# Picking expert numbers for four heads at once, with halving additions on GpSimd, in a hybrid decoder block

## The chip, the core and the metric

The kernel runs on one core of a Trainium2 chip. The core has five engines with a queue of instructions each: TensorE (PE in the views, with PEld for its weight loads), VectorE (DVE), ScalarE (ACT), GpSimd (POOL) and SyncE (SP, which here only issues DMAs). Each queue is worked off in order; the engines wait for one another at semaphores. The metric is the time of one execution on the device in microseconds, as the median of several runs. Before the change it is 3037.69 us (three runs, 3037.05 to 3041.81).

## What is computed

One decoder block over 16 meta tokens and 1024 tokens of width 1024: a convolution branch and a latent attention branch, joined by a projection, and then a PEER layer, which mixes 128 x 128 = 16384 experts. The change is in the PEER layer, which works on chunks of 128 tokens (C = 128):

```python
def one(xb):
    q = (xb @ wq).reshape(C, PEER_HEADS, 2, PEER_DK_HALF)              # 8 heads
    s = jnp.einsum('chpd,hpnd->chpn', q, keys)                         # 2 x 128 key scores
    sv, si = lax.top_k(s, 16)
    cand = sv[:, :, 0, :, None] + sv[:, :, 1, None, :]
    cidx = si[:, :, 0, :, None] * N_KEYS + si[:, :, 1, None, :]
    top_s, sel = lax.top_k(cand.reshape(C, PEER_HEADS, 256), 16)
    eidx = jnp.take_along_axis(cidx.reshape(C, PEER_HEADS, 256), sel, axis=-1)
    g = jax.nn.softmax(top_s, axis=-1)
    u = u_tab[eidx]
    act = jax.nn.gelu(jnp.einsum('chkd,cd->chk', u, xb), approximate=False)
    return jnp.einsum('chk,chkd->cd', g * act, v_tab[eidx])
```

Every token so uses 8 x 16 = 128 rows of u_tab and of v_tab, and `eidx` holds their numbers.

## The kernel before

The 1024 tokens are eight chunks of 128, in groups SC of 1, 1, 2, 2 and 2 chunks. A hand-written list of steps, ORDER, sets the order in which the code is written: B is attention of a group, C its output projection and key scores (`mix_out`), S the pick of experts (`select`), T the turning of their numbers and weights (`turn`), E an expansion (`expand`), G and the loop D the rest. A scheduler then orders the instructions of each engine anew, by that order as priority and by its own estimate of when operands and buffers are there. So a change in one place can move instructions in others.

**select** (L610 to L655) works on one chunk. Of the 256 sums of two scores only 50 can be among the best 16 (NCAND; the first 8 are among NC1 = 20), and they are laid out as `cand`, with their expert numbers as `cidx`. DVE finds the best 16 and their places among the 50. To turn a place into an expert number, L631 to L639 go over the heads one by one (HB = 1) and over two halves of the 16: DVE compares the 8 places with 0 to n-1, which gives a one-hot tile `eq` (L637, 20 x 8 or 50 x 8 elements of f16); POOL multiplies it by `cidx` into `ep` (L638); DVE sums over the candidates into `ef` (L639). That is 16 of each of the three per chunk, with two buffers for each tile.

Chunks 0 to 3 (GATHER) then fetch the picked rows: `gather_u` issues 128 indirect DMAs per chunk on POOL's queue, a row for each token into `ug` (three buffers, L688), and DVE multiplies each with the tokens `xn` and sums (L691, written as ujunk). `gather_v` does the same with v_tab into `vg` (seven buffers, L714), four at a time, and PE adds each four, weighted, by 16 matmuls into `gv` (L718, a "step" below, 32 for each chunk). The sum is added to the stream `ht` and normalised by `finish`. All these are written late (steps G32 and D0), and the scheduler draws them forward into free places.

Chunks 4 to 7 (DENSE) are instead multiplied with all experts. `expand` (L739 to L769) makes a 128 x 128 table of weights per token: DVE writes one-hot tiles `two` and `one` (L753, L754) of 8 tokens, then the products `ah` (L755) and `al` (L756), the latter in every other round on POOL (ALP); PE multiplies them into `pg` (L761, L762), ACT copies to `st` (L764), and DMAs write the table `g_d`. There are 16 rounds per chunk. `one` has a single buffer, so the next round's `one` waits until `al` has read it; the others have two.

The loop of `dense` (L810 to L835) takes four rows of experts in each of 32 groups: PE multiplies u (`pa`) and v (`pv`), 96 matmuls each per group (pv goes to `acc` by L835), and after each row of experts some of the gather is written in (RATE). At the end `finish` normalises chunks 4 to 7.

## Time and profile before

| what | value |
|---|---|
| median of three runs | 3037.69 us |
| profiled execution, its own time | 3034.4 us |
| its span, first to last instruction | 3032.6 us |
| granted PE clock, mean over the span | 0.908 |
| PE busy, of the span | 85% |
| DVE busy | 71% |
| POOL busy | 52% |
| ACT busy | 33% |
| bytes moved by DMA | 858 MB, 283 GB/s |

All rows that are read below come from that one execution, so a sum is made against 3034.4 us and then carried to the median. In the views, a row of an engine names the line of code, the operation, the tile written and the tiles read, the shape, and a count; times are us, the durations of single instructions ns. Busy time of overlapping instructions is counted once. "Waits" are idle time of an engine, put down to what ended it.

### The profile page before, as it was taken

The numbers are of one execution on the slowest core, as the hardware profiler recorded it, in microseconds if no ns is written. First come the engines' busy times: TensorE is split into PE (matmuls) and PEld (weight loads), VectorE is DVE, ScalarE is ACT, GpSimd is POOL, SyncE is SP. The second block draws the span as 40 slices with busy tenths as digits, with TensorE's granted clock in tenths as the row PEclk, the third lists the DMA queues.
The fourth block names the chain that finished last, engine by engine and source line by source line (L and its number), as shares of the span: only waits on it lengthen the run. The fifth ranks groups of instructions, "written<-read, shape, count | busy, mean of one in ns | idle before, by whom it ended". The sixth has DMA issues, their size and how long they took to land.

```text
span 3032.6 us, 40483 instructions
## 1 busy us (share of the span) xinstructions
PE 2591.0 (85%) x13295; PEld 1932.6 (64%) x13295; DVE 2165.6 (71%) x4917; ACT 1009.9 (33%) x2200; POOL 1589.2 (52%) x1608
## 2 busy tenths in 40 slices
PE   6878669897876756558998999999999999999996
PEld 6775547776643534336877777777777777776663
DVE  4888857999998999876877766666676656653332
ACT  5435325352520433443222222322232322232221
POOL 5885453534568668662333544544555444534444
PEclk9888858898897877668999999999999999999998
DMA  4114789896788996998888999999999999978886
GB/s 141 46 49 144 227 257 322 261 295 225 246 280 288 314 305 228 315 307 316 300 297 285 326 356 348 332 347 335 346 334 345 337 343 339 352 282 318 311 308 215
DMA packets 372563, 858.36 MB, mean 283 GB/s; under 512 B 37952, under 2 KB 134400, under 8 KB 368256
## 3 DMA queue, kind: packets, MB, share of 16 engines
q0 software_dynamic: 147456, 536.94, 50.9%
q1 hardware_dynamic: 216528, 295.68, 28.7%
q10 hardware_dynamic: 8368, 23.15, 2.1%
q8 instruction: 105, 1.72, 0.2%
q14 instruction: 106, 0.87, 0.1%
HBM read 798.92 MB, written 56.71 MB: 282 GB/s over the span
## 4 chain that ended last, share of the span: by engine, by line
PE 49%; DVE 17%; DMA 12%; issue 4%; POOL 3%; ACT 1%; POOLq 0%; DVEq 0%; ACTq 0%; SPq 0%
PE pv L178 19%; PE pa L178 18%; DMA ug<-in_dram,ei 9%; PE gv L718 7%; DVE ujunk L691 4%; DVE ef L639 2%; DMA vg<-in_dram,eT 1%; PE op L564 1%; DVE two L753 1%; DVE eq L637 1%; DVE ah L755 1%; POOL vg L714 1%; DVE one L754 1%; POOL ug L688 1%; POOL al L756 1%
## 5 line engine op out<-in xcount | busy, mean ns | idle before, releaser
L714 POOL DMA_INDIRECT vg<-in_dram,eT x512 | 559.5, 1093 | 652.6 <-PE gv L718 520.0
L688 POOL DMA_INDIRECT ug<-in_dram,ei x512 | 553.7, 1081 | 584.4 <-DVE ujunk L691 299.6
L691 DVE SCALAR_TENSOR_TENSOR ujunk<-ug,xn 128x1024 bf16<-128x1024 f32 x512 | 638.4, 1247 | 149.4 <-DMA ug<-in_dram,ei 139.1
L835 DVE TENSOR_TENSOR acc<-acc,pv 128x512 f32<-128x512 f32 x256 | 171.9, 685 | 203.5 <-PE pv L178 176.1
L718 PE MATMUL gv<-vg,wd 128*32 128x512 f32 x2048 | 275.6, 653 | 37.5 <-DMA vg<-in_dram,eT 37.4
L178 PE MATMUL pv<-v_0h,wh 128*128 128x512 f32 x512 | 201.3, 398 | 23.9 <-ACT wh L821 16.9
L178 PE MATMUL pv<-v_1l,wh 128*128 128x512 f32 x512 | 200.9, 394 | 3.7 <-DVE v_1l L784 3.7
L178 PE MATMUL pa<-xdh,u_1l 128*128 128x512 f32 x512 | 200.8, 392 | 2.5 <-DVE u_1l L784 2.5
L178 PE MATMUL pa<-xdh,u_0h 128*128 128x512 f32 x512 | 202.1, 395 | 0.3 <-ACT st L764 0.3
L178 PE MATMUL pa<-xdl,u_0h 128*128 128x512 f32 x512 | 201.3, 393 | 0.0
L178 PE MATMUL pa<-xdh,u_0l 128*128 128x512 f32 x512 | 201.2, 393 | 0.0
L178 PE MATMUL pa<-xdh,u_1h 128*128 128x512 f32 x512 | 201.0, 393 | 0.2 <-ACT u_1h L783 0.2
L178 PE MATMUL pa<-xdl,u_1h 128*128 128x512 f32 x512 | 200.4, 391 | 0.0
L178 PE MATMUL pv<-v_0l,wh 128*128 128x512 f32 x512 | 200.3, 395 | 0.0
L178 PE MATMUL pv<-v_1h,wl 128*128 128x512 f32 x512 | 199.9, 392 | 0.0
L178 PE MATMUL pv<-v_1h,wh 128*128 128x512 f32 x512 | 196.5, 396 | 2.8 <-DVE acc L835 2.8
L783 ACT ACTIVATE u_1h<-u_1r 128x512 fp32r<-128x512 f32 x128 | 80.7, 631 | 349.6 <-PE pa L178 251.1
L178 PE MATMUL pv<-v_0h,wl 128*128 128x512 f32 x512 | 194.7, 395 | 0.8 <-DVE wl L822 0.8
L764 ACT ACTIVATE st<-pg 128x256 f32<-128x256 f32 x256 | 130.1, 644 | 190.0 <-PE pg L762 140.7
L783 ACT ACTIVATE u_0h<-u_0r 128x512 fp32r<-128x512 f32 x128 | 80.8, 631 | 322.4 <-PE pa L178 244.9
L761 PE MATMUL pg<-ah,two 128*128 128x128 f16 x512 | 98.0, 271 | 98.2 <-DVE ah L755 82.8
L784 DVE TENSOR_TENSOR u_0l<-u_0r,u_0h 128x512 fp32r<-128x512 f32 x128 | 88.5, 692 | 126.6 <-ACT u_0h L783 89.7
(449 smaller groups left out, 5910.1 us busy)
## 6 DMA issues: line engine op xcount, KB each, us to landing
g_d<-st SPq DMA_DIRECT2D x32, 1024.0 KB
u_0r<-in_dram SPq DMA_DIRECT2D x128, 256.0 KB
u_1r<-in_dram SPq DMA_DIRECT2D x128, 256.0 KB
gt<-g_d SPq DMA_DIRECT2D x32, 1024.0 KB
v_0r<-in_dram SPq DMA_DIRECT2D x128, 256.0 KB
v_1r<-in_dram SPq DMA_DIRECT2D x128, 256.0 KB
wo<-in_dram SPq DMA_DIRECT2D x80, 256.0 KB
wq<-in_dram SPq DMA_DIRECT2D x80, 256.0 KB
```

Of the source, the lines that this page charges most:

```text
L178: PE.matmul(dst, l, r, start=first and j == 0, stop=last and j == 2)
L564: PE.matmul(pb, MT[:, k, j * P:(j + 1) * P], w[k // 2][:, k % 2], start=k == 0, stop=k == KD - 1)
L639: V.tensor_reduce(e[:, h:h + HB, ks], pr.rearrange("p h c k -> p h k c"), axis=AX.X, op=OP.add)
L688: G.indirect_dma_start(out=ug, out_offset=None, in_=u_tab, in_offset=bass.IndirectOffsetOnAxis(ap=ei[:, j:j + 1], axis=0))
L691: V.scalar_tensor_tensor(junk, ug, 1.0, xn, op0=OP.mult, op1=OP.mult, accum_out=dots[:, j:j + 1])
L714: G.indirect_dma_start(out=vg[j], out_offset=None, in_=v_tab, in_offset=bass.IndirectOffsetOnAxis(ap=eT[:, t:t + 1], axis=0))
L718: PE.matmul(acc[32 * j:32 * j + 32, 512 * n:512 * n + 512], w[:, j, 32 * i:32 * i + 32], vg[j][:, 512 * n:512 * n + 512], start=q == 0 and ...
L761: PE.matmul(pg[:, k], two[:, a, :, b], ah[:, a, :, b], start=True, stop=False)
L764: A.activation(st[i][:, :, r0 + r:r0 + r + 4].rearrange("p a b -> p b a"), pg[:, :, i * NK // 2:(i + 1) * NK // 2], AF.Copy, scale=1.0 / G ...
L783: A.activation(hi, raw, AF.Copy)
L784: V.tensor_tensor(lo, raw, hi.bitcast(F32), op=OP.subtract)
L835: V.tensor_tensor(a, a, pv, op=OP.add)
```

## The change

`select` takes a number of heads at a time from `dim.hb`: 1 for chunk 0 as before, 4 for the others. For these, a tile holds 4 x 20 x 8 or 4 x 50 x 8 elements and has one buffer (`dim.eb`). After the multiplication POOL folds the candidates: it adds the upper half onto the lower while more than 13 are left, so 20 become 10 by one addition and 50 become 25 and then 13 by two. DVE sums the remaining 10 or 13. Per chunk there are 4 comparisons, 4 multiplications, 6 additions and 4 reductions. In `expand` the tile `one` gets a second buffer.

```diff
-        for h in range(0, H, HB):
+        hb = dim.hb
+        for h in range(0, H, hb):
             for i, n in enumerate((NC1, NCAND)):
                 ks = slice(8 * i, 8 * i + 8)
-                sh = [P, HB, n, 8]
-                eq = sel.tile(sh, F16, name=f"eq{c}_{h}_{i}", tag=f"eq{i}", bufs=2)
-                pr = sel.tile(sh, F32, name=f"ep{c}_{h}_{i}", tag=f"ep{i}", bufs=2)
-                V.tensor_tensor(eq, tf[:, h:h + HB, None, ks].broadcast_to(sh), iota_c[:, None, :n].broadcast_to(sh), op=OP.is_equal)
-                G.tensor_tensor(pr, eq, cidx[:, h:h + HB, :n, None].broadcast_to(sh), op=OP.mult)
-                V.tensor_reduce(e[:, h:h + HB, ks], pr.rearrange("p h c k -> p h k c"), axis=AX.X, op=OP.add)
+                sh = [P, hb, n, 8]
+                eq = sel.tile(sh, F16, name=f"eq{c}_{h}_{i}", tag=f"eq{i}", bufs=dim.eb)
+                pr = sel.tile(sh, F32, name=f"ep{c}_{h}_{i}", tag=f"ep{i}", bufs=dim.eb)
+                V.tensor_tensor(eq, tf[:, h:h + hb, None, ks].broadcast_to(sh), iota_c[:, None, :n].broadcast_to(sh), op=OP.is_equal)
+                G.tensor_tensor(pr, eq, cidx[:, h:h + hb, :n, None].broadcast_to(sh), op=OP.mult)
+                while hb > 1 and n > 13:
+                    m = n // 2
+                    G.tensor_tensor(pr[:, :, :m], pr[:, :, :m], pr[:, :, n - m:n], op=OP.add)
+                    n -= m
+                V.tensor_reduce(e[:, h:h + hb, ks], pr[:, :, :n].rearrange("p h c k -> p h k c"), axis=AX.X, op=OP.add)
...
-                                    for n, b in (("one", 1), ("two", 2), ("ah", 2), ("al", 2))]
+                                    for n, b in (("one", 2), ("two", 2), ("ah", 2), ("al", 2))]
...
-    dim = SimpleNamespace(nw=1, nk=1, wraw=WRAW0)
+    dim = SimpleNamespace(nw=1, nk=1, wraw=WRAW0, hb=1, eb=2)
...
-    dim = SimpleNamespace(nw=NW, nk=NC, wraw=WRAW)
+    dim = SimpleNamespace(nw=NW, nk=NC, wraw=WRAW, hb=H // 2, eb=1)
```

In the changed kernel the multiplication stands in L638, the additions in L641, the reduction in L643; other lines of the profile before are one lower above these and four higher below (the ug issue is L692, the vg issue L718, the products of `expand` L757 to L760).

The scheduler makes of this the following. POOL's queue at the pick of chunk 4, before (ep and eq are named by head and half, ug and vg by the row that they fetch; the last number is the buffer's):

```order
L638 TENSOR_TENSOR ep_0_0_7299<-eq_0_0_7298,cidx_7229 128x160
L638 TENSOR_TENSOR ep_0_1_7304<-eq_0_1_7303,cidx_7229 128x400
L638 TENSOR_TENSOR ep_1_0_7309<-eq_1_0_7308,cidx_7229 128x160
L638 TENSOR_TENSOR ep_1_1_7314<-eq_1_1_7313,cidx_7229 128x400
L714 DMA vg_101_12419<-in_dram,eT_2889 128x1024
L714 DMA vg_6_12489<-in_dram,eT_2889 128x1024
L714 DMA vg_38_12491<-in_dram,eT_2889 128x1024
L638 TENSOR_TENSOR ep_2_0_7319<-eq_2_0_7318,cidx_7229 128x160
L714 DMA vg_70_12493<-in_dram,eT_2889 128x1024
L688 DMA ug_22_12437<-in_dram,ei_4618 128x1024
L638 TENSOR_TENSOR ep_2_1_7324<-eq_2_1_7323,cidx_7229 128x400
```

and the same queue at the same pick after:

```order
L638 TENSOR_TENSOR ep_0_0_7137<-eq_0_0_7136,cidx_7067 128x640
L638 TENSOR_TENSOR ep_0_1_7143<-eq_0_1_7142,cidx_7067 128x1600
L692 DMA ug_22_12059<-in_dram,ei_4564 128x1024
L641 TENSOR_TENSOR ep_0_0_7137<-ep_0_0_7137 128x4x80
L692 DMA ug_23_12063<-in_dram,ei_4564 128x1024
L641 TENSOR_TENSOR ep_0_1_7143<-ep_0_1_7143 128x4x200
L718 DMA vg_103_12193<-in_dram,eT_2889 128x1024
L718 DMA vg_8_12264<-in_dram,eT_2889 128x1024
L718 DMA vg_40_12266<-in_dram,eT_2889 128x1024
L718 DMA vg_72_12268<-in_dram,eT_2889 128x1024
L692 DMA ug_24_12127<-in_dram,ei_4564 128x1024
L641 TENSOR_TENSOR ep_0_1_7143<-ep_0_1_7143 128x4x96
```

Before, a multiplication is all that a reduction needs of POOL; after, the last addition of a half stands behind seven more issues.

DVE's queue in the expansion of chunk 7, before (one, two, ah and al are named by quarter of the chunk and first token of the round; L691 is the product of a gathered row):

```order
L754 TENSOR_TENSOR one_2_0_11083<-io,gd_10258 128x1024
L753 TENSOR_TENSOR two_2_0_11084<-io,gd_10258 128x1024
L755 TENSOR_TENSOR ah_2_0_11085<-one_2_0_11083,gd_10258 128x1024
L756 TENSOR_TENSOR al_2_0_11086<-one_2_0_11083,gd_10258 128x1024
L753 TENSOR_TENSOR two_2_8_11114<-io,gd_10258 128x1024
L691 SCALAR_TENSOR_TENSOR ujunk,dots_12008<-ug_79_13950,xn_12006 128x1024
L754 TENSOR_TENSOR one_2_8_11113<-io,gd_10258 128x1024
L753 TENSOR_TENSOR two_2_16_11144<-io,gd_10258 128x1024
L755 TENSOR_TENSOR ah_2_8_11115<-one_2_8_11113,gd_10258 128x1024
L754 TENSOR_TENSOR one_2_16_11143<-io,gd_10258 128x1024
```

and after:

```order
L758 TENSOR_TENSOR one_1_24_10671<-io,gd_9880 128x1024
L758 TENSOR_TENSOR one_2_0_10705<-io,gd_9880 128x1024
L757 TENSOR_TENSOR two_1_24_10672<-io,gd_9880 128x1024
L759 TENSOR_TENSOR ah_1_24_10673<-one_1_24_10671,gd_9880 128x1024
L695 SCALAR_TENSOR_TENSOR ujunk,dots_11630<-ug_90_13958,xn_11628 128x1024
L758 TENSOR_TENSOR one_2_8_10735<-io,gd_9880 128x1024
L695 SCALAR_TENSOR_TENSOR ujunk,dots_11630<-ug_91_13962,xn_11628 128x1024
L695 SCALAR_TENSOR_TENSOR ujunk,dots_11630<-ug_92_13982,xn_11628 128x1024
L759 TENSOR_TENSOR ah_2_0_10707<-one_2_0_10705,gd_9880 128x1024
```

The tile one is now written a round ahead, and the gather is eleven rows further at the same place.

The end of DVE's queue, before (L724 adds the last gathered chunk to ht, L736 normalises):

```order
L784 TENSOR_TENSOR v_3_1l<-v_3_1r,v_3_1h 128x512
L835 TENSOR_TENSOR acc<-acc,pv_1_0_26309 128x512
L835 TENSOR_TENSOR acc<-acc,pv_1_1_26323 128x512
L835 TENSOR_TENSOR acc<-acc,pv_1_2_26337 128x512
L835 TENSOR_TENSOR acc<-acc,pv_1_3_26351 128x512
L724 TENSOR_TENSOR ht_25387<-ht_25387,gv_22294 128x1024
L736 SCALAR_TENSOR_TENSOR ht_25387<-ht_25387,os_25391,gfin 128x1024
L736 SCALAR_TENSOR_TENSOR acc<-acc,os_26366,gfin 128x1024
```

and after:

```order
L822 TENSOR_TENSOR ge_25820<-ge_25820,gt_25649 128x512
L728 TENSOR_TENSOR ht_25009<-ht_25009,gv_21916 128x1024
L826 TENSOR_TENSOR wl_25824<-ge_25820,wh_25823 128x512
L740 SCALAR_TENSOR_TENSOR ht_25009<-ht_25009,os_25013,gfin 128x1024
L839 TENSOR_TENSOR acc<-acc,pv_0_0_25851 128x512
L839 TENSOR_TENSOR acc<-acc,pv_0_1_25865 128x512
L839 TENSOR_TENSOR acc<-acc,pv_0_2_25879 128x512
```

The last gathered chunk is finished ahead of the last group's eight additions to acc, where it stood behind them. On PE the last three steps of gv stood behind the last pv; now 96 pv stand behind the last gv.

## Rows read from the trace of the kernel before

**Rows 1.** The page: busy us, share of the span, instructions of each engine

```profile
PE 2591.0 (85%) x13295; PEld 1932.6 (64%) x13295; DVE 2165.6 (71%) x4917; ACT 1009.9 (33%) x2200; POOL 1589.2 (52%) x1608
```

**Rows 2.** Busy time by stretch: us, engines (instructions), PE clock, DMA share, GB/s

```profile
735.00:800.00 65.00, 56.08 (x278) 44.52 (x276) 65.00 (x204) 26.48 (x74) 44.54 (x58) 0.87 0.65 206
875.00:1000.00 125.00, 72.81 (x347) 43.39 (x348) 109.47 (x374) 15.93 (x37) 104.55 (x119) 0.77 0.83 289
1100.00:1217.00 117.00, 63.08 (x395) 41.42 (x395) 115.82 (x351) 38.93 (x76) 91.36 (x98) 0.69 0.81 271
1217.00:1365.00 148.00, 79.17 (x629) 49.37 (x629) 117.06 (x165) 62.56 (x125) 95.40 (x72) 0.64 0.93 309
...
1400.00:1760.00 360.00, 339.29 (x1471) 267.34 (x1472) 285.44 (x479) 103.96 (x185) 143.83 (x130) 0.99 0.87 302
1760.00:2990.00 1230.00, 1228.16 (x6019) 890.22 (x6021) 712.61 (x1146) 341.86 (x573) 579.78 (x539) 1.00 0.92 330
```

**Rows 3.** Groups by line and shape: busy us, mean ns, idle before and releaser

```profile
L638 POOL TENSOR_TENSOR ep<-eq,cidx 128x400 f32<-128x400 f16 x64 | 60.2, 944 | 15.1 <-DVE eq L637 14.8
...
L639 DVE TENSOR_REDUCE ef<-ep 128x8 f32<-128x400 f32 x64 | 55.4, 865 | 0.7 <-POOL ep L638 0.7
...
L638 POOL TENSOR_TENSOR ep<-eq,cidx 128x160 f32<-128x160 f16 x64 | 44.9, 703 | 18.4 <-DVE eq L637 17.5 <-DVE tv L604 0.3 <-DVE gs L645 0.2
...
L637 DVE TENSOR_TENSOR eq<-tf,iota_c 128x160 f16<-128x160 f16 x64 | 32.5, 507 | 0.0
...
L639 DVE TENSOR_REDUCE ef<-ep 128x8 f32<-128x160 f32 x64 | 27.3, 428 | 5.7 <-POOL ep L638 5.7
...
L637 DVE TENSOR_TENSOR eq<-tf,iota_c 128x400 f16<-128x400 f16 x64 | 26.3, 411 | 0.0
```

**Rows 4.** POOL's float sums and products, lines L327, L341: minimum, median, maximum ns

```profile
L327 POOL TENSOR_TENSOR first<-first,ct x60: 443/460/1477, 39.8 to 192.5; 128x128 f32<-128x128 f32 x60
...
L341 POOL TENSOR_TENSOR y<-y,gln x8: 1265/1293/2358, 204.8 to 343.9; 128x512 f32<-128x512 f32 x8
```

**Rows 5.** Timeline, DVE, 1284 to 1298 us: start, us, instruction [idle before, releaser]

```profile
1292.34 0.69 DVE L754 TENSOR_TENSOR one<-io,gd 128x1024 f16<-128x1024 f16 x1 [6.49 <-POOL al L756]
...
1293.55 0.68 DVE L755 TENSOR_TENSOR ah<-one,gd 128x1024 f16<-128x1024 f16 x1
...
1297.10 2.37 DVE L755 TENSOR_TENSOR ah<-one,gd 128x1024 f16<-128x1024 f16 x1
```

**Rows 6.** Timeline, POOL, 1284 to 1299 us

```profile
1286.96 0.94 POOL L714 DMA_INDIRECT vg<-in_dram,eT  x1 [0.30 <-issue]
...
1290.40 1.91 POOL L756 TENSOR_TENSOR al<-one,gd 128x1024 f16<-128x1024 f16 x1
1296.21 2.72 POOL L756 TENSOR_TENSOR al<-one,gd 128x1024 f16<-128x1024 f16 x1 [3.90 <-DVE one L754]
```

**Rows 7.** Waits, 1217 to 1365 us: engine and line, for what; us, times, longest

```profile
DVE one L754 <- POOL al L756: 26.0, 5, 7.0
```

**Rows 8.** Waits, 1400 to 1760 us

```profile
DVE ujunk L691 <- DMA ug<-in_dram,ei: 61.6, 40, 7.3
```

**Rows 9.** Chain that ended last, 2950 to 3033 us: start, us, what

```profile
2982.03 7.07 PE pv L178 x30
2989.10 1.98 PE gv L718 x16
...
2991.21 4.14 DMA vg<-in_dram,eT
...
2997.57 5.36 DMA vg<-in_dram,eT
...
3006.87 5.14 DMA vg<-in_dram,eT
...
3015.49 1.23 DVE ht L724
...
3026.07 1.28 DVE acc L736
```

More of the change, by code (lines that the diff above doesn't have):

```diff
@@ L51 @@
 NC1 = sum(na * nb for _, na, _, nb in BLOCKS[:4])
-HB = 1
 SC = [(0, 128), (128, 128), (256, 256), (512, 256), (768, 256)]
```

## The prediction

> **What bounds the kernel now.** I read the page first: PE is busy for 85% of the span, VectorE (DVE) for 71%, ScalarE (ACT) for 33% and GpSimd (POOL) for 52% [rows 1]. Such shares mix stages, so the second view is busy time by stretch [rows 2]. From 1760 to 2990 us PE is busy for 1228 of 1230 us at a granted clock of 1.00 (the 2.4 GHz level): there only fewer or shorter matmuls help, and the change removes none of them. The picture before that is another. In 735 to 800 us, where experts of chunks 2 and 3 are picked, DVE has no idle time at all; in 1100 to 1217 us (chunks 6 and 7) it is busy for 115.8 of 117 us; in 875 to 1000 us (chunks 4 and 5) DVE has 109.5 and POOL 104.6 of 125 us, so both are near their limit. In 1217 to 1365 us (the last two expansions into one-hot tiles) no engine is full: DVE and POOL wait for each other. The third view is the groups by line and shape, for what the changed lines cost [rows 3]; the fourth the timelines of DVE and POOL in one expansion round [rows 5, 6]; the last is the end of the chain [rows 9].
>
> **Part 1, picks for four heads at once, on DVE.** Per chunk, before: eight reductions of 160 elements at 428 ns and eight of 400 at 865 ns [rows 3], 10.3 us. The two sizes give (865 - 428)/240 = 1.82 ns an element and a fixed 137 ns. After: two of 320 elements (4 x 10 x 8) and two of 416 (4 x 13 x 8), 0.72 and 0.89 us, together 3.2 us. That is 7.1 us a chunk; chunk 0 keeps the old form, so seven chunks give 50 us. The comparisons cost 8 x (507 + 411) ns = 7.3 us a chunk [rows 3]. After, there are four of 640 and 1600 elements. A free one of 1024 elements of f16 takes 0.68 us [rows 5], and with 411 ns at 400 that makes 0.51 and 0.93 us, 2.9 us a chunk: 31 us less in all. But a two-input DVE instruction that meets a GpSimd one waits for it: the same 1024-element product takes 0.68 us at 1293.55 and 2.37 us at 1297.10, while the 2.72 us POOL product that began at 1296.21 runs [rows 5, 6]. The multiplications that the new comparisons meet are longer (below, 1.3 and 2.8 us). If each of the four meets one in full, 8.2 us a chunk come on top, and the comparisons cost 27 us more than before. I take the middle of these means, half a multiplication each on average: 4.1 us a chunk, 2 us gained in all, and keep +31 and -27. DVE so loses between 23 and 81 us of work; I take 52.
>
> The Trainium skill (SBUF — State Buffer, section "Who interferes with whom") says of the pair of ports which VectorE and GpSimd share that a VectorE instruction with two SBUF inputs contends with a GpSimd instruction that reads SBUF, and that reductions never do on trn2. By that rule the work moves from instructions which are never blocked to additions that block others, and the time would be that of the second rival; the pair of products at 1293.55 and 1297.10 agrees with the rule.
>
> **On POOL.** Before, 8 x (703 + 944) ns = 13.2 us a chunk [rows 3]. After, two multiplications of 640 and two of 1600: from 944 ns at 400 elements and 1.91 us at 1024 [rows 3, 6] 1.55 ns an element, 1.3 and 2.8 us, 8.2 us a chunk. No halving addition stands in the trace; the nearest are other float adds and products in SBUF, 443 ns at 128 elements and 1265 ns at 512 at their fastest [rows 4], 2.14 ns an element. Each half then takes 0.86 us (320), 1.88 (800) and 0.99 (384): 7.5 us a chunk. In sum 15.7 us, 2.5 more than before, 18 us over seven chunks; at the slowest row (2.36 us for 512, 1.9 times) 66 us. I take 30, nearer to the fast end, since DVE blocks less often with fewer instructions.
>
> **What of it is on the path.** Where DVE was full, POOL becomes the next bound: 735 to 800 us had 44.5 us of POOL work and gets some 9 more, 53 of 65; 875 to 1000 us gets 113 of 125; 1100 to 1217 us 100 of 117 [rows 2]. Idle POOL time gone entirely, these give back 12, 12 and 17 us, and chunk 1 perhaps 1: at most 42 us. If DVE stays the bound all of its 52 to 81 us counts; if POOL's waits for gathers stay as they are, nothing does. Reductions hardly wait for POOL now (5.7 and 0.7 us in 128 times [rows 3]); after, each waits for a chain of one multiplication and one or two additions, with gathers in between: in the GpSimd table the second addition of the first half stands behind four vg and three ug issues. I take 30 us off.
>
> **Part 2, the second one tile.** In 1217 to 1365 us DVE waits 26.0 us in 5 places for POOL's product before it may overwrite one [rows 7]; one of them is the 6.49 us before 1292.34 [rows 5], while POOL does four vg issues of 0.94 us, 0.3 us apart, before its product [rows 6]. The buffer takes this wait away, 26 us at most. What comes next is POOL itself, busy for 95.4 of 148 us [rows 2] plus about 54 gaps of 0.3 us, 111 us. And the scheduler uses the room: counted in the order, 68 gathers stand between the 17th and the last POOL product of the expansions where 54 stood. 14 x 1.24 us = 17 us more, 129 of 148. DMA engines are at 0.93 there, 309 GB/s [rows 2]; 14 x 0.52 MB at that rate would be 24 us by itself. So between 19 us faster and 24 us slower; I take 4 faster, since the DMA engines moved 330 GB/s at 0.92 in 1760 to 2990 us, and the wait is there in the trace.
>
> **Part 3, what the pulled-forward gathers give at the end.** This is the largest sure term. Before, three of the gather's matmul steps (16 matmuls each) stand behind the last pv: PE waits 4.14, 5.36 and 5.14 us for their rows, then ht is added, and five normalisations follow [rows 9]. From the step that starts at 2989.10 us to the end of the span are 43.5 us. After, by the order, all gv stand before the last 96 pv, and ht of chunk 3 is finished ahead of them. What is left from the same point is PE work: four steps at 1.9 us and 15 pv at 7.07/30 us [rows 9], 11 us; then the finish. Now 10.6 us lie between ht and the last of five products and 6.5 us from that product's start to the end; two of the five are left to do then, 4 and 6.5, 10.5 us. 43.5 - 21.5 is 22 us; one more step of 1.9 us is already done before the dense loop (32 instead of 31). Total 24 us. 96 pv at 0.236 us are 22.6 us, enough to cover the 17 us from ht to the end. If the gather rows come later than the order assumes, the waits return inside the loop and as little as 8 us is left.
>
> In 1400 to 1760 us PE has 339 of 360 us, for DVE waits 61.6 us for ug rows [rows 2, 8]. Counted in the order, DVE has 98 ug to take in the first six groups of the dense loop after, and 108 in the first seven before, so the same share is lost: I count nothing.
>
> **Sum.** The profiled execution took 3034.4 us with a span of 3032.6. 3034.4 - 30 - 4 - 24 = 2976. It lies 3.3 us under the median of the runs shown (3037.69), so the forecast is 2980 us.
>
> **Rivals.** (1) **Reductions wait for POOL**, slower. 28 reductions stand in DVE's in-order queue; behind each stand the products with xn (ujunk) that free the ug buffers, and the one-hot products that PE and ACT wait for. For: the chain in the GpSimd table, two multiplications, three additions and seven issues, is some 16 us long. Against: between the second comparison of that half and its reduction the order puts 33 rows of other DVE work, and today POOL waits for DVE, not the other way. DVE saves 52; with a wait w each the stages change by 28w - 52, and the tail gives back 24, so it decides from w = 2.7 us. At 4 us: 3034 + 60 - 24 + 3 = 3073; at 3.2 us 3052. (2) **POOL's longer work blocks DVE**: every comparison and many ujunk and one-hot products wait; DVE saves 23 instead of 52, the path perhaps 5. 3034 - 5 - 24 + 3 = 3008. Rows 5 and 6 speak for it; against it, blocking is there already (160 elements take 507 ns by mean, 400 take 411 [rows 3]) in 112 comparisons, and 28 are left. (3) **DVE remains the bound throughout**: 60 from the picks, 15 from the one tile, 24 at the end: 2938. For: DVE full in three stretches; against: POOL's 104.6 of 125. (4) **Gathers pulled forward are paid where they are put**, DMA at its limit in 1217 to 1365 us: 20 to 24 us lost there, the tail and nothing else gained: 3034 to 3040, no change.
>
> **Chances.** Forecast (2955 to 3000) 0.52, blocking (3000 to 3028) 0.16, DVE bound (below 2955) 0.13, no change 0.09, waits 0.10. The range 2942 to 3035 leaves out the far halves of the third and first rival. A measurement of this kernel tells about 0.2%, 6 us. Faster 0.81, same 0.09, slower 0.10.
>
> **What would show it.** In the profile after: reductions x28 near 0.7 and 0.9 us; additions near 0.9, 1.9 and 1.0 us; little idle time before L643 on POOL's account (much of it: rival 1); comparisons near 0.5 and 0.9 us (2 us and more: rival 2); no DVE wait of 6 us before one; PE full from 1360 to 1375 us on, not from 1400; and no gv between the last pv and the end. The prediction is wrong if the dense loop comes no earlier, or if PE waits for vg in the last 100 us.

## The result and the profile after

The changed kernel takes 3058.99 us (median of 6 runs), the kernel before 3042.47 us (6 runs beside it): ratio 1.0062, 95% interval 1.0049 to 1.0076. That is **slower** by 17 us by the medians and 19 us by the ratio: small, but clear of the noise. The forecast was 2980 us and faster; the range ended at 3035. For most single instructions and at the end of the program the forecast held; what failed lies between 560 and 1480 us. The two profiled executions differ by 22 us, a little more than the medians.

The page after, busy us of each engine (as [rows 1]):

```profile
PE 2590.0 (85%) x13295; PEld 1930.5 (63%) x13295; DVE 2179.4 (71%) x4749; ACT 1011.4 (33%) x2200; POOL 1605.6 (53%) x1566
```

VectorE has 168 instructions fewer and is busy for 14 us *longer*. The changed lines alone do not say why. Groups by line and shape of the kernel after, as [rows 3]: busy us, mean ns, idle before and releaser.

```profile
L638 POOL TENSOR_TENSOR ep<-eq,cidx 128x1600 f32<-128x1600 f16 x14 | 44.4, 3170 | 1.7 <-DVE ef L643 1.6
...
L641 POOL TENSOR_TENSOR ep<-ep 128x800 f32<-128x800 f32 x14 | 27.5, 1964 | 0.3
L638 POOL TENSOR_TENSOR ep<-eq,cidx 128x640 f32<-128x640 f16 x14 | 21.2, 1512 | 5.5 <-DVE eq L637 2.9 <-DVE mx L503 1.8 <-DVE ef L643 0.6
L637 DVE TENSOR_TENSOR eq<-tf,iota_c 128x1600 f16<-128x1600 f16 x14 | 18.0, 1287 | 2.4 <-POOL ep L638 2.4
L641 POOL TENSOR_TENSOR ep<-ep 128x384 f32<-128x384 f32 x14 | 15.8, 1126 | 0.2
L637 DVE TENSOR_TENSOR eq<-tf,iota_c 128x640 f16<-128x640 f16 x14 | 12.6, 902 | 4.2 <-POOL ep L638 4.2
L643 DVE TENSOR_REDUCE ef<-ep 128x32 f32<-128x416 f32 x14 | 12.5, 893 | 8.0 <-POOL ep L641 8.0
L641 POOL TENSOR_TENSOR ep<-ep 128x320 f32<-128x320 f32 x14 | 12.3, 877 | 0.2
L643 DVE TENSOR_REDUCE ef<-ep 128x32 f32<-128x320 f32 x14 | 10.0, 713 | 0.0
```

Most prices of the forecast are met here: reductions 0.71 and 0.89 us, additions 0.88, 1.96 and 1.13 (0.86, 1.88 and 0.99 were forecast). Multiplications are some 15% longer than forecast, 1.51 and 3.17 us for 1.3 and 2.8, and comparisons, at 0.90 and 1.29, lie between the free price of 0.51 and 0.93 and the longer one that was taken. The reductions wait 8.0 us in all for POOL, so the first rival is out. The same kind of row for the dot products `ujunk`, from 560 to 1430 us, before and then after:

```profile
L691 DVE SCALAR_TENSOR_TENSOR ujunk<-ug,xn 128x1024 bf16<-128x1024 f32 x175 | 226.1, 1292 | 22.3 <-DMA ug<-in_dram,ei 20.5 <-issue 0.8 <-DVE sx L605 0.7
```

```profile
L695 DVE SCALAR_TENSOR_TENSOR ujunk<-ug,xn 128x1024 bf16<-128x1024 f32 x183 | 272.3, 1488 | 49.0 <-DMA ug<-in_dram,ei 47.2 <-issue 1.3
```

A line that the change does not touch: its mean rose from 1292 to 1488 ns, and the idle time ahead of it from 22 to 49 us, on the account of the gathers. Together these are 73 us, of which some 10 are eight more of them; the reductions and comparisons saved 50 and 19 us. The timelines show one of these instructions. First VectorE (DVE), then POOL, kernel after, around 591 us (start, us, instruction):

```profile
591.16 5.14 DVE L695 SCALAR_TENSOR_TENSOR ujunk<-ug,xn 128x1024 bf16<-128x1024 f32 x1
596.24 0.08 DVE L695 DVE_READ_ACCUMULATOR ujunk<-ug,xn 128x1 f32 x1
```

```profile
591.32 0.86 POOL L641 TENSOR_TENSOR ep<-ep 128x320 f32<-128x320 f32 x1
592.14 0.18 POOL L139 TENSOR_TENSOR fs<-fs,pow_c 128x1 f32<-128x1 f32 x1
592.29 2.92 POOL L638 TENSOR_TENSOR ep<-eq,cidx 128x1600 f32<-128x1600 f16 x1
596.59 0.99 POOL L692 DMA_INDIRECT ug<-in_dram,ei  x1 [1.37 <-DVE ujunk L695]
```

A free `ujunk` takes 1.22 us; this one is held for the whole of an addition and of the four-head multiplication behind it, although it began first, and ends 1.1 us after them. The next gather is issued only then: it waits 1.37 us for the buffer that `ujunk` gives back. So VectorE loses twice, once held and once waiting for rows that were asked for late.

Busy time by stretch after (columns as [rows 2]; the third line, which ended with the expansions at 1365 us, now runs to 1412 us, and its work is not the same: the last reduction of the picks starts at 1277.6 us, where it started at 1216.8 before):

```profile
875.00:1000.00 125.00, 74.07 (x356) 44.74 (x356) 98.05 (x317) 12.91 (x31) 98.24 (x95) 0.77 0.76 255
1100.00:1217.00 117.00, 61.60 (x468) 41.94 (x466) 113.87 (x374) 45.19 (x94) 79.68 (x62) 0.70 0.88 289
1217.00:1412.00 195.00, 106.30 (x749) 67.76 (x750) 162.99 (x213) 70.67 (x141) 147.35 (x119) 0.65 0.89 294
1400.00:1760.00 360.00, 321.99 (x1404) 256.68 (x1403) 282.15 (x471) 106.76 (x191) 130.82 (x120) 0.96 0.87 299
1760.00:2990.00 1230.00, 1224.75 (x6001) 883.58 (x6000) 704.35 (x1131) 340.45 (x570) 574.90 (x541) 1.00 0.93 333
```

The last accumulation of the dense loop's first group stands at 1438.6 us before and 1483.2 after (L835, L839): 44.6 us late. The loop then takes 1556.7 and 1562.9 us to its last accumulation. The wait of `one` fell as meant ([rows 7], 26.0 us in 5 places), and the wait for `ug` in the loop's first part is as before ([rows 8], 61.6 us in 40). Waits, 1217 to 1412 us and 1400 to 1760 us, kernel after:

```profile
DVE one L758 <- POOL al L760: 8.1, 4, 2.8
```

```profile
DVE ujunk L695 <- DMA ug<-in_dram,ei: 62.5, 43, 3.6
```

The end behaves as forecast: the last step of `gv` starts at 3019.90 us, ahead of the last 96 `pv`, and one accumulation and its normalisation are all that follow the loop (timeline of PE, then two pieces of the chain that ended last; compare [rows 9]).

```profile
3019.90 1.92 PE L722 MATMUL gv<-vg,wd 128*32 128x512 f32 x16
```

```profile
3045.43 0.69 DVE acc L839
...
3048.31 1.28 DVE acc L740
```

From the last accumulation to the end of the span 37.3 us became 8.7.

### The profile page after: what moved, and what is told of

It is laid out like the page before. It is cut to its first block, busy times and chain, and to the rows that moved or that the text cites. A ratio compares the mean times of both kernels' runs of the same rounds, so it can differ in the third digit from the quotient of the medians.

```text
span 3054.9 us, 40224 instructions
## 1 busy us (share of the span) xinstructions
PE 2590.0 (85%) x13295; PEld 1930.5 (63%) x13295; DVE 2179.4 (71%) x4749; ACT 1011.4 (33%) x2200; POOL 1605.6 (53%) x1566
## 5 line engine op out<-in xcount | busy, mean ns | idle before, releaser
L718 POOL DMA_INDIRECT vg<-in_dram,eT x512 | 558.5, 1091 | 673.6 <-PE gv L722 534.5
L692 POOL DMA_INDIRECT ug<-in_dram,ei x512 | 553.8, 1082 | 577.8 <-DVE ujunk L695 308.6
L695 DVE SCALAR_TENSOR_TENSOR ujunk<-ug,xn 128x1024 bf16<-128x1024 f32 x512 | 674.2, 1317 | 168.8 <-DMA ug<-in_dram,ei 159.1
L839 DVE TENSOR_TENSOR acc<-acc,pv 128x512 f32<-128x512 f32 x256 | 171.9, 684 | 197.9 <-PE pv L177 167.2
L722 PEld LDWEIGHTS gv<-vg,wd 128*32 128x32 f32 x2048 | 57.3, 116 | 207.7 <-issue 143.3
```

The source lines that it names most:

```text
L692: G.indirect_dma_start(out=ug, out_offset=None, in_=u_tab, in_offset=bass.IndirectOffsetOnAxis(ap=ei[:, j:j + 1], axis=0))
L695: V.scalar_tensor_tensor(junk, ug, 1.0, xn, op0=OP.mult, op1=OP.mult, accum_out=dots[:, j:j + 1])
L718: G.indirect_dma_start(out=vg[j], out_offset=None, in_=v_tab, in_offset=bass.IndirectOffsetOnAxis(ap=eT[:, t:t + 1], axis=0))
L722: PE.matmul(acc[32 * j:32 * j + 32, 512 * n:512 * n + 512], w[:, j, 32 * i:32 * i + 32], vg[j][:, 512 * n:512 * n + 512], start=q == 0 and ...
L839: V.tensor_tensor(a, a, pv, op=OP.add)
```

## The experiments

All ratios are against the kernel before on the same chip. "Loop" is the end of the loop's first group in us, "end" the time from the last accumulation to the end of the span, "u" the dot products that the order puts ahead of the first accumulation. The last three columns split VectorE's time from the first comparison of chunk 1 to "loop". *Held* is what its instructions took over the free time of their kind (the lower quartile of the same operation, tiles and shape over all these traces), counted from 0.15 us on; *idle* is time with no instruction; *work* is the rest. All columns but the ratio come from the profiled run of each kernel.

| kernel | ratio (95%) | loop | end | u | work | held | idle |
|---|---|---|---|---|---|---|---|
| before | 1 | 1438.6 | 37.3 | 221 | 691 | 71 | 107 |
| after | 1.0062 (1.0049-1.0076) | 1483.2 | 8.7 | 237 | 663 | 132 | 117 |
| 1 picks only | 1.0025 (1.0012-1.0038) | 1478.4 | 8.7 | 232 | 662 | 103 | 145 |
| 2 `one` only | 0.9927 (0.9902-0.9951) | 1439.9 | 18.3 | 223 | 693 | 80 | 97 |
| 3 grouping only | 0.9910 (0.9887-0.9933) | 1414.7 | 37.6 | 218 | 678 | 63 | 104 |
| 4 additions left out | 0.9886 (0.9864-0.9909) | 1410.6 | 33.4 | 219 | 641 | 78 | 122 |
| 5 one input | 1.0030 (1.0016-1.0044) | 1472.7 | 8.8 | 234 | 664 | 77 | 161 |
| 6 iota | 0.9960 (0.9945-0.9976) | 1458.4 | 8.8 | 229 | 657 | 74 | 157 |
| 7 additions on VectorE | 0.9920 (0.9901-0.9939) | 1437.5 | 24.9 | 221 | 665 | 97 | 100 |
| 8 grouping and `one` | 0.9932 (0.9915-0.9948) | 1433.4 | 32.7 | 219 | 676 | 80 | 96 |
| 9 short products on VectorE | 0.9946 (0.9930-0.9962) | 1429.1 | 29.8 | 221 | 684 | 72 | 96 |
| 10 gathers held | 1.0047 (1.0029-1.0065) | 1471.2 | 24.6 | 220 | 646 | 132 | 118 |
| 11 iota, held | 0.9992 (0.9974-1.0010) | 1456.9 | 24.4 | 220 | 646 | 92 | 144 |
| 12 iota twice, held | 1.0054 (1.0036-1.0071) | 1452.2 | 24.6 | 220 | 649 | 87 | 147 |
| 13 additions twice, held | 1.0197 (1.0171-1.0223) | 1516.6 | 20.6 | 221 | 649 | 159 | 137 |

The profiled run of kernel 12 was 14 us under the median of its runs, so its times in us are too small by up to that; its ratio is the better figure. That of the kernel before and that of kernel 13 were 8 us under their medians, kernel 1's 7 us over; the others lie within some 5 us.

**1 and 2: each part alone.** Edits against the kernel after (1) and before (2):

```diff
-                                    for n, b in (("one", 2), ("two", 2), ("ah", 2), ("al", 2))]
+                                    for n, b in (("one", 1), ("two", 2), ("ah", 2), ("al", 2))]
```

```diff
-                                    for n, b in (("one", 1), ("two", 2), ("ah", 2), ("al", 2))]
+                                    for n, b in (("one", 2), ("two", 2), ("ah", 2), ("al", 2))]
```

> The changed selection alone, the one-hot tile `one` with one buffer as before. Theory (GpSimd's additions and four-head products hold up VectorE's instructions that read two SBUF tiles, above all the dot products ujunk, and the 20 gathers that the order pulls ahead of the dense loop are paid there): the loss is the selection's, so about 0 to +25 us against the kernel before (the whole change lost 16.5), the dense loop starting 25 to 50 us later, the stretch after the last accumulation short (10 to 15 us, before 37), and ujunk, two, ah at 40 to 60 us more busy time than their free durations before the dense loop. Rival (the second buffer of `one` costs): -10 to -30 us, as the selection gains what was forecast.

> The second buffer of `one` alone, the selection as before. Theory (the selection makes the loss): -10 to +5 us against the kernel before; waits of `one` on `al` gone (26 us in the expansion before), most of them taken up by the next instructions. Rival (the second buffer brings the loss, by letting one-hot and products of two batches run against each other): +10 to +25 us.

The picks alone cost 0.25%, 8 us; the second buffer alone *gains* 0.73%, 22 us. Neither of its two expectations had that. It gains at the end, not in the expansions: the loop starts as before (1439.9), but one step of `gv` instead of three then stands behind the last `pv`, and the end falls from 37 to 18 us. The whole change has that shorter end from the picks already (8.7 us in both), so the gain is not there a second time; with the picks the buffer costs 0.37%, 11 us. (Held time is where this shows: 103 us for the picks alone, 132 with the buffer.)

**3 and 4: the grouping without the additions.** Kernel 3 takes the additions out and reduces all candidates on VectorE; kernel 4 leaves the additions out and keeps the short reductions. Both have `one` as before.

```diff
-                while hb > 1 and n > 13:
-                    m = n // 2
-                    G.tensor_tensor(pr[:, :, :m], pr[:, :, :m], pr[:, :, n - m:n], op=OP.add)
-                    n -= m
```

```diff
                 while hb > 1 and n > 13:
                     m = n // 2
-                    G.tensor_tensor(pr[:, :, :m], pr[:, :, :m], pr[:, :, n - m:n], op=OP.add)
                     n -= m
```

> Four heads at a time, without any addition: VectorE's reductions read all 20 and 50 candidates, `one` with one buffer. VectorE's comparisons cost some 19 us less than before and its reductions about the same (68 against 72 us), 218 dot products ahead of the loop. Theory (the additions on GpSimd make the loss): first group of the loop ends 0 to 20 us earlier than before's 1438.6, and the time is -15 to +5 us. Rival (the long four-head multiplications make it): +10 to +25 us.

> As the run with the changed selection alone, but GpSimd's additions are left out, so that the reductions sum only the first 10 or 13 of the candidates' products: the picked numbers are not the reference's. VectorE's work is that of the changed selection, GpSimd has about 56 us less than in it. Theory (additions hold up VectorE): VectorE's excess over free durations before the dense loop falls from about 130 us to 70 to 90, the dense loop starts 10 to 40 us earlier than in the kernel before, the end stays as long as before (no gather is pulled ahead), so -10 to -40 us. Rival (the four-head products and the order, not the additions, make the loss): the dense loop starts no earlier than in the kernel before, 0 to +20 us.

Grouping alone is the better half of the change: 0.9910, 27 us faster than the kernel before, and more than either of its expectations allowed. Its multiplications are 29 us shorter in sum on POOL than before and its comparisons shorter on VectorE. The additions are the loss: with them 1.0025, without them 0.9886, 42 us. What they were added for is worth little. Kernel 3's groups by line and shape:

```profile
L639 DVE TENSOR_REDUCE ef<-ep 128x32 f32<-128x1600 f32 x14 | 42.7, 3049 | 0.0
...
L639 DVE TENSOR_REDUCE ef<-ep 128x32 f32<-128x640 f32 x14 | 18.3, 1308 | 3.2 <-POOL ep L638 3.2
```

The long reductions cost 61 us there and 22 us with the additions, and kernel 4, which has the short ones for nothing, is only 0.24% faster than kernel 3, within their intervals. From kernel 3 to kernel 4 work falls by 37 us, and held and idle time together rise by 33.

**5 and 6: what GpSimd reads.** In place of each addition stands an instruction that reads one tile, or none:

```diff
-                    G.tensor_tensor(pr[:, :, :m], pr[:, :, :m], pr[:, :, n - m:n], op=OP.add)
+                    G.tensor_scalar(pr[:, :, :m], pr[:, :, :m], 1.0, None, op0=OP.mult)
```

```diff
-                    G.tensor_tensor(pr[:, :, :m], pr[:, :, :m], pr[:, :, n - m:n], op=OP.add)
+                    G.iota(pr[:, :, :m], pattern=[[0, hb], [0, m], [1, 8]], base=0, ...)
```

> As the run with the changed selection alone, but each addition on GpSimd is a multiplication of the first part by 1.0 in place, one SBUF tile read instead of two, with the same waits: the sum is left out, so the picked numbers are not the reference's. The order of the instructions and the pulled gathers are close to those of the changed selection (234 dot products ahead of the first accumulation, against 232). Theory (GpSimd's two-input instructions hold up VectorE): VectorE's excess over free durations falls by 25 to 50 us against the run with the changed selection alone and the time by 15 to 40 us. Rival (order and pulled gathers make the loss): the same time as the changed selection alone, within 8 us. Third: GpSimd's instruction holds VectorE up with one input as well, then excess and time stay, if it lasts as long.

> As the run with the changed selection alone, but each addition on GpSimd is an iota into the same tile, which reads nothing: the sum is left out, so the picked numbers are not the reference's. The order stays near that of the changed selection alone (229 dot products ahead of the first accumulation, against 232). An iota of 400 elements took 0.83 us before, so 800, 384 and 320 elements take about 1.66, 0.80 and 0.66, in all some 44 us against 57 for the additions. Theory A (what holds VectorE up is GpSimd reading SBUF): VectorE's excess over free durations falls from 103 to 60 to 75 us and the first group of the dense loop ends at 1410 to 1435, against 1478. Theory B (after the one-input run: it is GpSimd's time ahead of the gathers on its own queue, and the gathers that the scheduler pulls ahead of the loop, whatever VectorE's excess is): the excess falls as well, but the first group ends at 1450 to 1472, and the time is 0 to 15 us under that of the changed selection alone.

With one input the held time fell from 103 to 77 us, as the theory of held instructions had it, but idle time rose by 16 us and the time did not fall. The stand-ins are longer, 68 us in all against 56, which explains only a part of it. One of their rows, kernel 5:

```profile
L641 POOL TENSOR_SCALAR ep<-ep 128x800 f32<-128x800 f32 x14 | 32.1, 2296 | 0.3
```

With the iota held time fell likewise, and the time by 0.65%, 20 us. The loop, at 1458.4, is where theory B had it; the time is 5 us better than that theory allowed. Against kernel 4, which has nothing in these places, the 43 us of iotas cost 0.74%, 22 us. Without the sums, kernels 5 and 6 fetch other rows, but not in less time: a `ug` gather lands in 6.5 us by median with the iota, 6.3 with the picks alone. They also had other numbers of gathers ahead of the loop, so I held these in place next.

**10: the pulled gathers.** Against the kernel after:

```diff
+            if c == GATHER[1] and j == HELD:
+                late = const.tile([P, P - HELD], I32, name="late", tag="late", bufs=1)
+                V.tensor_tensor(late, ei[:, HELD:], zero[0].broadcast_to([P, P - HELD]), op=OP.add)
...
+                if ci == 3 and q == 3 and r0 == TG - TH:
+                    zero.append(const.tile([P, 1], I32, name="zero"))
+                    V.tensor_scalar(zero[0], ah[:, 0, 0, 0:1], 0.0, None, op0=OP.mult)
```

From `HELD` = 83 on the gathers read `late`. Busy time from 560 us to "loop", of the kernel before, after, and this one (columns as [rows 2]):

```profile
560.00:1438.60 878.60, 621.49 (x3558) 447.71 (x3557) 771.46 (x2362) 319.61 (x780) 530.32 (x532) 0.81 0.85 283
```

```profile
560.00:1483.20 923.20, 628.88 (x3581) 451.03 (x3580) 806.40 (x2245) 321.82 (x784) 585.33 (x517) 0.80 0.85 283
```

```profile
560.00:1471.20 911.20, 630.96 (x3604) 456.09 (x3603) 792.10 (x2234) 321.58 (x786) 571.28 (x511) 0.80 0.84 279
```

> The whole change, with one more condition: the dot products from number 211 on (the second gathered chunk from its column 83) take their row numbers from a copy that is made only after the last one-hot product. So 220 dot products stand ahead of the first accumulation, as in the kernel before (221), against 237; up to there the order of every engine is that of the change. Theory B, with the transfers as the price (560 us to the end of the loop's first group carried 248.9 MB before and 261.0 after, at 283 GB/s both): 17 gathers of 0.52 MB fewer are 8.9 MB, 31 us, so the first group ends near 1452 (1444 to 1462), the end of the program grows to 18 to 35 us, and the total is within 12 us of the change's. What is left of 1452 against 1438.6 is GpSimd's additions. Rival (the pulled gathers lie in time that is idle anyway, and the whole 45 us are the additions'): the first group ends at 1475 to 1487, and the total is 10 to 25 us above the change's.

The loop came 12 us earlier, between both expectations, and the loop itself got 6 us shorter; the end took 16 us back, 24.6 against 8.7. The total is that of the change (1.0047, 1.0062, overlapping). This is the end of the held kernel's chain, with the wait for gathered rows and the late `ht` of [rows 9] again:

```profile
3026.39 5.36 DMA vg<-in_dram,eT
...
3035.51 1.23 DVE ht L733
```

So what the fourth rival says of the total is right: gathers pulled ahead of the loop are paid there (12 and 6 us) and give the same back (16 us). My price of 31 us for their transfers, at 283 GB/s, was more than double: the DMA rate fell to 279 GB/s when bytes were taken away, so the bytes were not the bound, here or in that rival. With the gathers in their old place the change still brings the loop 33 us later than before.

**11, 12 and 13: queue time or held time.** On top of kernel 10: an iota for each addition, each iota twice, each addition twice (the second into the half that is read no more).

```diff
+                    G.iota(pr[:, :, :m], ...)
+                    G.iota(pr[:, :, :m], ...)
```

```diff
                     G.tensor_tensor(pr[:, :, :m], pr[:, :, :m], pr[:, :, n - m:n], op=OP.add)
+                    G.tensor_tensor(pr[:, :, n - m:n], pr[:, :, n - m:n], pr[:, :, :m], op=OP.add)
```

> The change with the gathers held, and each addition replaced by an iota into the same tile, which reads nothing (43 us in place of 56; the sum is left out, so the picked numbers are not the reference's). The same 211 and 220 dot products and 256 second-table products as with the gathers held, so the pulled gathers play no part. Theory Q (GpSimd's own time on its queue counts, 0.5 to 0.8 us for each): 6 to 11 us under the kernel with the gathers held. Theory S (what counts is VectorE held up while GpSimd reads SBUF, excess 130 there): the excess falls to 70 to 80 and the time by 20 to 35 us.

> The same with each iota issued twice (about 86 us; the sum is left out, so the picked numbers are not the reference's). Theory Q: 20 to 35 us above the kernel with one iota. Theory S: within 8 us of it, with the same excess of VectorE.

> The change with the gathers held and each addition followed by a second one of the same size into the half that is read no more (about 112 us of additions in place of 56; the outputs stay those of the reference). Theory Q: 28 to 45 us above the kernel with the gathers held, as much for each us of GpSimd as the iotas. Theory S: more for each us than the iotas, in step with VectorE's excess: 30 to 60 us of excess more, 25 to 50 us of time. The two part at the iotas, here only by the ratio.

Neither theory alone fits. The second set of iotas, 44 us of POOL time, costs 0.62%, 19 us: POOL's own time counts, some 0.4 us for each us, which speaks against theory S. The second set of additions, 51 us, costs 1.50%, 46 us, 0.9 us for each us, twice as much as iotas. And additions in place of iotas cost 0.55%, 17 us, for 13 us more of POOL time. The traces show both costs. Where the iota stands, a `ujunk` that runs beside it keeps its 1.2 us; VectorE, then POOL, kernel 12:

```profile
826.25 1.20 DVE L701 SCALAR_TENSOR_TENSOR ujunk<-ug,xn 128x1024 bf16<-128x1024 f32 x1
```

```profile
826.57 0.83 POOL L643 IOTA ep<- 128x384 f32 x1
```

Sorted by the kind of POOL instruction (gather issues left out) that a held VectorE instruction overlaps most, the additions hold VectorE for 33 us after, 29 us with the picks alone, 34 us with the gathers held and 70 us when doubled; the one-input stand-ins 11 us, the iotas 1 to 5 us. The multiplications hold it for some 30 us before (47 instructions) and 47 us after (20): fewer and longer. The products `al` on POOL, which the change does not touch, hold it for 40 us before, 30 us with the picks alone, 51 us with the second buffer alone and 52 us after. So the 61 us more of held time are about 33 of additions, 17 of multiplications and 12 of `al`. Where two kinds overlap one instruction the sorting is a choice: by the single instruction that overlaps longest the additions come to 24 us after. What the iotas cost instead is idle time, for late gathers and, doubled, late reductions: POOL's time reaches VectorE on both ways. Waits, 560 to 1430 us, before, then kernels 11 and 12:

```profile
DVE ujunk L691 <- DMA ug<-in_dram,ei: 20.5, 13, 4.3
...
DVE ef L639 <- POOL ep L638: 6.4, 4, 5.1
```

```profile
DVE ujunk L700 <- DMA ug<-in_dram,ei: 37.9, 24, 5.7
...
DVE ef L645 <- POOL ep L643: 6.5, 4, 3.0
```

```profile
DVE ujunk L701 <- DMA ug<-in_dram,ei: 51.6, 35, 9.7
DVE ef L646 <- POOL ep L644: 32.3, 9, 7.2
```

**7, 8 and 9: other places for the same work.** The whole change with `V.` for `G.` in the additions; the whole change without the additions; and that with the short multiplications on VectorE.

```diff
-                    G.tensor_tensor(pr[:, :, :m], pr[:, :, :m], pr[:, :, n - m:n], op=OP.add)
+                    V.tensor_tensor(pr[:, :, :m], pr[:, :, :m], pr[:, :, n - m:n], op=OP.add)
```

```diff
-                G.tensor_tensor(pr, eq, cidx[:, h:h + hb, :n, None].broadcast_to(sh), op=OP.mult)
+                (G if i else V).tensor_tensor(pr, eq, cidx[:, h:h + hb, :n, None].broadcast_to(sh), op=OP.mult)
```

> The whole change, but with its additions on VectorE in place of GpSimd. Additions of 800, 384 and 320 elements cost VectorE 2.0 us together by its rows on two fp32 tiles (256 elements 0.42, 1024 elements 1.27), 29 us in all; GpSimd loses 56. 221 dot products and 256 second-table products ahead of the loop, as with the second buffer alone. Theory B (GpSimd's time and the gathers that it brings ahead): first group ends at 1425 to 1445, the end as with the second buffer alone (about 18 us), -20 to -40 us against the kernel before. Rival (the grouping or the second buffer makes the loss, wherever the additions run): +5 to +20 us.

> Four heads at a time and the second buffer of `one`, no addition: VectorE's reductions read all candidates. 219 dot products and 248 second-table products ahead of the loop, so the end of the program is the long one of the kernel before. Theory B (GpSimd's time in the stretch ahead of the loop, 29 us less multiplication than before, is what counts there): first group ends at 1408 to 1420, the end 33 to 38 us, -20 to -32 us against the kernel before, no better than grouping alone. Rival (both gains add, 26 and 22): -40 to -50 us.

> As the kernel with four heads at a time and the second buffer of `one`, without additions, and the 14 multiplications of 640 elements run on VectorE (about 0.9 us each, 13 us) in place of GpSimd (1.5 us each, 20 us). Theory B (GpSimd's queue is what counts, VectorE's 46 us shorter reductions were worth 4): first group ends 0 to 15 us earlier than with that kernel. Rival (VectorE is as much the bound as GpSimd): 5 to 15 us later.

The very additions of the change, on VectorE (0.67, 0.98 and 0.55 us each for 320, 800 and 384 elements), turn 1.0062 into 0.9920: it was their engine, not their number, that lost. Grouping and second buffer together (0.9932) are no better than either alone; why the gains do not add was not tested. And 17 us less on POOL for 21 us more on VectorE change nothing (0.9946 against 0.9932). The best version that computes all sums is grouping alone.

## Why the prediction was wrong

- **The picks on VectorE: sizes right.** The reductions cost what was forecast; the comparisons are held less often than I took. They saved 50 and 19 us in the trace (forecast 50 and 2). A slip beside it: comparisons that each meet a multiplication in full come to 26 us more, not 27.
- **The picks on POOL: right.** Additions and multiplications take 121 us in the stretch against 95, 26 more; 30 were taken. (The multiplications came out longer than forecast, and the margin for slow additions covered it.)
- **What of it is on the path: the step that failed.** I bounded how much POOL would hold up VectorE by the comparisons alone, each meeting a multiplication. Left out of the bound were the additions, on the side of what holds, and all other VectorE instructions with two SBUF inputs, on the side of what is held. Measured: the comparisons' held time fell from 17 to 10 us, that of `ujunk` rose from 14 to 49, of all from 71 to 132, 33 of it by the additions. VectorE's time splits as 691 + 71 + 107 us before and 663 + 132 + 117 after, so of the 28 us less work nothing is left; with the gathers in their old place it is 646 + 132 + 118: 45 us less work, 61 more held, 12 more idle. In place of 30 us off stand 28 us on, in a kernel that has the second buffer too; the picks alone have 29 less work, 32 more held and 38 more idle. The loop then comes 45 us later, which the prediction itself named as a sign of being wrong.
- **Cover.** I credited VectorE's savings where VectorE was full, up to the point at which POOL fills. But the two are coupled both ways: a `ujunk` frees the buffer for the next gather, which POOL issues, on whose rows the next `ujunk` waits; the rows at 591 us show one turn of this ring. So idle POOL time was no free room: iotas, which hardly hold VectorE, still cost 0.4 us for each us, through late gathers and late reductions.
- **The second buffer: sign right alone, not in company.** The forecast was 4 us off (-19 to +24). Alone it gave 22 us off, in the tail and not in the expansions where I looked; with the picks it costs 11. The wait that I wanted away did go, but other VectorE instructions were held longer by `al`. (Of the four `vg` issues that I read as 0.94 us the first took 1.44.)
- **The end: right.** Forecast 24 us, measured 28.6 (37.3 to 8.7). But I counted the gathers that make it as free where they go. Kernel 10 puts 17 of them back: that takes 16 us of the tail away and gives 18 us back ahead of it and in the loop, so of this part nothing was left. The other 13 us of the tail stay in kernel 10; whether they too were paid elsewhere was not tested.
- **The rivals.** The first, waiting reductions, did not happen (8.0 us). The second, POOL blocks VectorE, named the mechanism, `ujunk` too, but priced it at 3008, by the comparisons; the fourth, pulled gathers paid where put, had the effect right and the reason, DMA at its limit, not borne out. What was measured is nearest to the two together, with the additions' hold and POOL's own time in the price: no rival combined them. (At 3.2 us the first rival's own sum gives 3051, not 3052.)
- The rule of the Trainium skill that the prediction weighed (SBUF — State Buffer, section "Who interferes with whom") agrees with these traces in kind: two-input additions on GpSimd hold two-input VectorE instructions (33 us), the iota, which reads nothing, hardly does (1 to 5 us), and the reductions kept their 0.71 and 0.89 us. How much is held the traces alone tell: one-input stand-ins, which read SBUF too, held VectorE for 11 us of their 68. I used the rule for a chance of 0.16.

What stays open: how the additions' 42 us divide exactly into held time and POOL's own time. At about 0.4 us for each us of POOL, the 56 us of additions come to some 24, and the rest would be held time; kernels 4, 6 and 1 give 22 for iotas in the same places and 20 more for additions. The two act on the same instructions, and single profiles differ by several us. Nor is it clear why the one-input stand-ins, with 26 us less held time, did not run faster: their 12 us more on POOL come to 5 at that price.

## What to carry to other kernels

When work goes from VectorE to GpSimd, look not at the instructions that move but at those that stay: list VectorE's long two-input instructions in the same stretch and bound their loss as if they met the new GpSimd work in full (here 56 us of additions held them for some 33). If GpSimd also issues the gathers that VectorE consumes, its time can be on the path although it is idle for a fifth or more of each stretch (here 27 of 125 us at the least). And a shorter tail that comes from work pulled forward is a gain only if the place that it is pulled to has room: put the same work back with one added dependency, and see whether the total moves.

## What was not expected of the hardware

A VectorE instruction that by its record starts 0.16 us ahead of a GpSimd addition is held all the same, through that addition and the multiplication behind it: 5.14 us in place of 1.22. A GpSimd product with a constant, one input, is longer than the two-input addition of the same 800 elements (2296 against 1964 ns), and yet these products hold VectorE about a third as much (11 against 29 us in sum, kernels 5 and 1).
